# Four steps of the neighbourhood attention moved from the second branch's products to the third branch's gates

## The chip, the cores and the metric

The kernel runs on one core of one Trainium2 chip. The metric is the device time of one execution in microseconds. The kernel before takes 856.8 us (median of three runs, 856.2 to 856.81). One more execution was recorded by the hardware profiler; it took 857.18 us, and its span, from the first to the last instruction, is 855.4 us.

## What is computed

One layer of an encoder block on a sequence of 512 tokens with 1024 channels, all in float32. A projection of the normalised input feeds three token mixers. The second and third of the reference's mixers, and the merge, are what matters here:

```python
h = rms_norm(x, mix_norm_g)
proj = h @ w_in                      # mLSTM q,k,v,o,gates | NA q,k,v | memory q | merge gates
y_ml = mlstm_branch(...)
y_na = neighbourhood_attention(na_q, na_k, na_v, na_rpb)   # 8 heads of 64, 8 x 64 token grid
y_xa = memory_cross_attention(xa_q, mem_k, mem_v)
gates = sigmoid(merge_pre + b_merge_gate)
merged = g_ml * (y_ml @ w_br_ml) + g_na * (y_na @ w_br_na) + g_xa * (y_xa @ w_br_xa)
x = x + merged @ w_out
x = x + conv_glu_ffn(rms_norm(x))    # then a final norm
```

The neighbourhood attention lets a token look at all 8 rows and at 16 columns around it: scores with a learned bias, a softmax, and a weighted sum of values.

## The kernel before

**The products.** TensorE multiplies in float32 by three matmuls per product (`mm3`, L360 to L362): high part by high part, high by low, and low by high. The splits into high and low parts are made by ScalarE (ACT, L326: the rounded copy) and VectorE (DVE, L327: the rest). `proj` makes one 128 x 512 output tile from eight such triples, k = 0 to 7, so 24 matmuls, and may call a function after any k (its argument `at`). Weights come from HBM by SyncE's queue (`wr`, L239) three blocks ahead of their use, and are split one block ahead.

**The branches.** The merge runs in three rounds of a loop over `br`: br = 0 the mLSTM, br = 1 the memory attention, br = 2 the neighbourhood attention. Each round makes eight gates (`gate`, a `proj` and a tanh on ACT, L1264) and eight branch products of 12 matmuls each (four pairs), which DVE multiplies by the gate and adds to the merge (L1286, L1287). In rounds 0 and 1 two gates and a pair of products take turns. In round 2 all eight gates come first, then `drain` empties the attention's queue, then all products, which read the attention's result (`yh`, `yl`).

**The attention's steps.** While a round's matmuls run, a generator is advanced bit by bit (`step`; `half` is one step here, except for the mLSTM). `na_all` is advanced in rounds 1 and 2. It works on 16 tiles (a head and half of the columns each), called tile 0 to 15 here, in 39 steps. Two steps are one turn t. The first step of turn t does, in the order of the code: the scores of tile t on TensorE (four matmuls of 256 columns, L989 and L990) with their softmax (DVE maximum L994, ACT exponential L999, DVE reciprocal L1000, ACT scaling L1002); the values of tile t - 3 (four matmuls, L1023) and their sum (`store`: ACT L1039, DVE L1040 and L1041; for every fourth tile also the split into `yh` and `yl`, L1045 and L1046); the split of tile t - 2 (`parts`: two ACT copies L1011 and two DVE rests L1012); and the load of the transposed tile t - 1 (`turn_in`, one DMA `U<-td` of SyncE's queue, L179). The second step transposes tile t within blocks on DVE (L170) and stores it to HBM by four DMAs (`turn_out`, `td<-s`, L173). After every fourth tile `prep` splits the next pair of heads (L965 to L969), and `load_vwin` brings its values by 32 DMAs of GpSimd (POOL, L669). So a tile's values stand three turns behind its scores, and in between lie its softmax, a store to HBM, a load, and a split.

**The order.** The code's order is not the program's. A scheduling layer builds the five engines' instruction streams and places an instruction by when it expects it to be ready; the engines then run their streams in order, and wait at semaphores. The tiles named `U` and the split tiles (`w` of L1011) share a pool of six buffers (`EB`). The sums `mm` have four banks of PSUM, the attention's `at` four others.

Before the change a step is taken after k = 3 and after k = 7 of each gate, and after each branch product. Rounds 1 and 2 hold 16 + 8 and 16 of these places, so 40, all 12 large matmuls apart.

Of the kernel before, what the change touches and what calls it, by code (L numbers as in the profile page):

```python
# [20 lines left out]
KT = D // P  # L21
# [109 lines left out]
def hybrid_block(ctx, tc, xT, memT, wflat, vecs, gbias, nabias, out):  # L131
# [18 lines left out]
    def unit(dt=F32):  # L150
        return up.tile([P, UNIT], dt, tag="unit", name=nm("u"))

    def scr(n=512):
        return sp.tile([P, 512], F32, tag="scr", name=nm("s"))[:, :n]
# [4 lines left out]
    def mmps():  # L159
        return mmp.tile([P, 512], F32, tag="mm", name=nm("mm"))  # L160

    def atps():
        return atp.tile([P, 512], F32, tag="at", name=nm("at"))
# [168 lines left out]
    def weights(key):  # L332

        i, _, n = BINDEX[key]
        last = len(BLOCKS) - 1
        while st["raw"] <= min(i + RAW_AHEAD, DOWN0 + NSP - 1):
            emit_raw(st["raw"])
            st["raw"] += 1
        while st["late"] <= min(i + 9, last if i >= DOWN0 else DOWN0 + NSP + 3):
            emit_raw(st["late"])  # L340
            st["late"] += 1
        while st["sum"] <= min(i + 8, st["late"] - 1):
            emit_sum(st["sum"])
            st["sum"] += 1
        while st["diff"] <= min(i + 3, last):
            emit_diff(st["diff"])
            st["diff"] += 1
        while st["split"] <= min(i + (2 if st["split"] >= DOWN0 else SPLIT_AHEAD), last):
            emit_split(st["split"])
            st["split"] += 1  # L350
        while st["form"] <= min(i + 3, last):
            emit_form(st["form"])
            st["form"] += 1
        while st["diff"] <= min(i + 4, last):
            emit_diff(st["diff"])
            st["diff"] += 1
        return split.pop(i)

    def mm3(ps, lh, ll, rh, rl, start, stop):
        PE.matmul(ps, lh, rh, start=start, stop=False)  # L360
        PE.matmul(ps, lh, rl, start=False, stop=False)  # L361
        st["mm"] = PE.matmul(ps, ll, rh, start=False, stop=stop).ins  # L362
# [152 lines left out]
    def proj(key, XHs, XLs, n=S, bank=None, at={}):  # L515
        ws = weights(key)
        ps = (bank or mmps)()
        for k in range(KT):
            mm3(ps[:, :n], ws[k][0], ws[k][1], XHs[k], XLs[k], k == 0, k == KT - 1)
            if k in at:  # L520
                at[k]()
        return ps
# [53 lines left out]
    for f in range(4):  # L576
        ps = ps_k[f] if f < 2 else proj(("mlk", f), XH, XL)
# [44 lines left out]
    NH = [xn[k // 4][:, (k % 4) * S:(k % 4 + 1) * S] for k in range(KT)]  # L622
    NL = [xn[2 + k // 4][:, (k % 4) * S:(k % 4 + 1) * S] for k in range(KT)]
# [13 lines left out]
    for c, n in enumerate(TMW):  # L637
        pss = [(mmps if c % 2 else atps)() for _ in range(NT)]
        g = 2 if n == 512 else 4
# [10 lines left out]
        for t in range(NT):  # L650
            ps = pss[t]
# [10 lines left out]
    def load_vwin(hp):  # L662

        vw = unit(F32R)
        for b in range(4):
            for hf in range(2):
                i = 2 * b + hf
                for r in range(4):
                    G.dma_start(vw[r * 32:(r + 1) * 32, i * 256:(i + 1) * 256],  # L669
                                nav_v[hf, r, CW[b]:CW[b] + 32, hp * 256:(hp + 1) * 256])  # L670
        return vw
# [494 lines left out]
    def step(n=1):  # L1166
        quota[0] += n
        while quota[0] >= 1 and gens:
            try:
                next(gens[0])  # L1170
                quota[0] -= 1
            except StopIteration:
                gens.pop(0)
        if not gens:
            quota[0] = 0.0

    def half():

        step(0.5 if gens and gens[0].__name__ == "ml_all" else 1)

    def mid(at={}):

        return {**at, 2: lambda: step(RB / 2)}
# [6 lines left out]
    for f in range(4):  # L1190
        ps = proj(("xaq", f), NH, NL, at=mid())
# [3 lines left out]
    for f in range(4):  # L1195
# [6 lines left out]
        ps = proj(("o", f), NH, NL, at=mid())  # L1202
        if f == 0:
            so.append(unit())
        g = so[0][:, f * S:(f + 1) * S]
# [29 lines left out]
    for f in range(4):  # L1235
        ps = proj(("naq", f), NH, NL, at=mid())
        A.activation(nq[:, f * S:(f + 1) * S].rearrange("p (b r c) -> p b r c", r=ROWS, b=4), rv(ps), AF.Copy)
        step(RB / 2)
    for f in range(4):
        ps = proj(("nak", f), NH, NL, at=mid())  # L1240
# [8 lines left out]
    def drain(names):  # L1249
        while any(g.__name__ in names for g in gens):  # L1250
            step(1)

    for br in range(3):
        gi = (0, 2, 1)[br]
        if br == 0:
            ys[1] = [unit(F32R), unit(F32R)]
            gens.append(xa_all(xq, mk, mv, *ys[1]))
        if br == 1:
            vw0 = load_vwin(0)
            ys[2] = [unit(F32R), unit(F32R)]  # L1260
            gens.append(na_all(nq, nk, vw0, *ys[2]))
        def gate(f, t):
            ps = proj(("g", br, f), NH, NL, at={3: half, KT - 1: half})
            A.activation(t, ps, AF.Tanh, scale=0.5, bias=mgbh[:, gi * 8 + f:gi * 8 + f + 1])  # L1264
            return t

        if br == 2:
            tgu = [unit(), unit()]
            tgs = [gate(f, tgu[f // 4][:, f % 4 * S:(f % 4 + 1) * S]) for f in range(KT)]
        for fp in range(4):  # L1270
            tg = tgs[2 * fp:2 * fp + 2] if br == 2 else [gate(2 * fp + i, scr()) for i in range(2)]
            drain(tags[br])
            if br == 0 and not mg:
                mg.extend([unit(), unit()])
            yh, yl = ys[br]
            ws = weights(("br", br, fp))
            for i in range(2):
                f = 2 * fp + i
                ps = mmps()
                for k in range(4):  # L1280
                    ks, fs = slice(k * S, (k + 1) * S), slice(i * P, (i + 1) * P)
                    mm3(ps, ws[k][0][:, fs], ws[k][1][:, fs], yh[:, ks], yl[:, ks], k == 0, k == 3)
                if br == 0:
                    V.scalar_tensor_tensor(mgv(f), tg[i], 1.0, ps, op0=ALU.add, op1=ALU.mult)
                else:
                    V.scalar_tensor_tensor(tg[i], tg[i], 1.0, ps, op0=ALU.add, op1=ALU.mult)  # L1286
                    V.tensor_tensor(mgv(f), mgv(f), tg[i], op=ALU.add)  # L1287
                half()
    mhu = [unit(F32R) for _ in range(4)]
    GH = [mhu[k // 4][:, (k % 4) * S:(k % 4 + 1) * S] for k in range(KT)]  # L1290
    GL = [mhu[2 + k // 4][:, (k % 4) * S:(k % 4 + 1) * S] for k in range(KT)]
# [10 lines left out]
    for f in range(KT):  # L1302
        xr = scr()
        SY.dma_start(xr, xT[:, f, :])
        ps = proj(("out", f), GH, GL)
# [14 lines left out]
    for f in range(FT):  # L1320
# [38 lines left out]
        if 3 <= f < 11:  # L1359
            t, g = (f - 3) % NT, (f - 3) // NT  # L1360
            turns[t, g] = turn_out(x2v[g][:, :, t * P:(t + 1) * P])
        if 6 <= f < 14:
            t, g = (f - 6) % NT, (f - 6) // NT
# [99 lines left out]
    for n, key in enumerate(DOWN):  # L1463
        wh, wl = weights(key)
        work(2 if len(todo) > 2 else 1)
        if key[0] == "s":
            _, i, p = key
# [14 lines left out]
        _, g, j = key  # L1482
# [18 lines left out]
        for t in range(NT):  # L1501
            tsl = slice(t * P, (t + 1) * P)
            for c in ((slice(0, HC),) if t < last else (slice(0, M), slice(M, HC))):
                end = c.start > 0
                ps = px[t] if t < last else atps()[:, :M]
# [118 lines left out]
```

## Time and profile before

| | |
|---|---|
| median of 3 runs | 856.8 us |
| profiled execution | 857.18 us, span 855.4 us |
| TensorE busy | 847.4 us (99% of the span), 4010 matmuls |
| DVE, ACT, POOL busy | 603.4, 455.2 and 150.8 us |
| TensorE's granted clock | 0.998 |
| tile 0's scores, tile 15's values | at 312.5 us and 426.8 us |
| round 2, gates | from about 379 us to 430 us |
| HBM traffic | 155 GB/s over the span |

The page gives for each engine how long it was busy; a matmul's record lasts longer than its distance to the next one, because matmuls overlap, so TensorE's true pace is read from the starts in the timeline. A view of the waits lists who held up whom; the timeline gives every instruction with its start, its duration, and in brackets the idle time before it. Everything that the change moves lies between 312 and 455 us.

### The profile page before, as it was taken

What the parts mean: (1) busy time and instruction counts of PE and PEld (TensorE: products, weight loads), DVE (VectorE), ACT (ScalarE), POOL (GpSimd) and SP (SyncE); (2) the same over time, 40 slices, a digit from 0 to 9 for tenths busy, and PEclk for the clock granted to TensorE, in tenths of its full rate; (3) what the DMA queues carried; (4) which work ended last, traced back from release to release, by engine and by line L of the source; (5) the groups of instructions that cost most, each with busy time, mean ns of one, the idle gap of its engine ahead of it and who ended that gap; (6) DMA issues with size and microseconds to landing.
All of it is one profiled execution on the core that took longest, in us unless ns stands there. A gap on an engine that the chain in (4) does not pass through costs nothing.

```text
span 855.4 us, 12106 instructions
## 1 busy us (share of the span) xinstructions
PE 847.4 (99%) x4010; PEld 711.8 (83%) x4010; DVE 603.4 (71%) x1194; ACT 455.2 (53%) x956; POOL 150.8 (18%) x236
## 2 busy tenths in 40 slices
PE   9999999999999999999999999999999999999997
PEld 7898988888888888888888888888888888888886
DVE  7699677865458658998586547767766677766773
ACT  7465557775446648887644334434444444533442
POOL 2000100000102830554000211211111111210211
PEclk9999999999999999999999999999999999999999
DMA  8236736563335846788523442544422223845842
GB/s 273 87 113 212 235 113 201 179 208 105 120 122 170 225 142 203 227 228 236 177 96 110 148 160 88 163 156 148 147 99 99 95 93 113 236 119 148 247 107 98
DMA packets 78158, 133.63 MB, mean 156 GB/s; under 512 B 10888, under 2 KB 38024, under 8 KB 78096
## 3 DMA queue, kind: packets, MB, share of 16 engines
q1 hardware_dynamic: 68144, 122.22, 44.2%
q0 software_dynamic: 9664, 10.51, 6.2%
q8 instruction: 31, 0.51, 0.2%
q14 instruction: 31, 0.25, 0.1%
q10 hardware_dynamic: 288, 0.14, 0.1%
HBM read 117.21 MB, written 15.62 MB: 155 GB/s over the span
## 4 chain that ended last, share of the span: by engine, by line
PE 98%; DMA 1%; issue 0%; ACT 0%; SPq 0%; DVE 0%; POOLq 0%; POOL 0%; ACTq 0%
PE mm L361 28%; PE mm L360 28%; PE mm L362 28%; PE at L360 3%; PE at L361 3%; PE at L362 3%; PE at L1023 1%; PE at L856 1%; PE at L858 1%; PE at L840 1%; DMA wr<-wflat 1%; PE at L990 0%; PE at L989 0%; PE at L800 0%; PE mm L542 0%
## 5 line engine op out<-in xcount | busy, mean ns | idle before, releaser
L360 PE MATMUL mm<-u,w 128*128 128x512 f32 x859 | 336.3, 391 | 0.0
L362 PE MATMUL mm<-u,w 128*128 128x512 f32 x859 | 335.0, 390 | 0.0
L361 PE MATMUL mm<-u,w 128*128 128x512 f32 x859 | 334.9, 390 | 0.0
L326 ACT ACTIVATE w<-wr 128x512 fp32r<-128x512 f32 (+1 forms) x256 | 159.6, 627 | 134.7 <-PE mm L362 96.9
L327 DVE TENSOR_TENSOR w<-wr,w 128x512 fp32r<-128x512 f32 (+2 forms) x257 | 177.7, 695 | 69.3 <-ACT w L326 67.1
L362 PEld LDWEIGHTS mm<-u,w 128*128 128x128 f32 x859 | 161.3, 188 | 33.9 <-DVE w L327 0.3
L360 PEld LDWEIGHTS mm<-u,w 128*128 128x128 f32 x859 | 161.5, 188 | 32.5
L361 PEld LDWEIGHTS mm<-u,w 128*128 128x128 f32 x859 | 161.5, 188 | 32.1
L669 POOL DMA_DIRECT2D u<-nav_d x128 | 62.0, 497 | 102.6 <-PE at L1023 51.7
L1344 POOL TENSOR_TENSOR s<-s,rb 128x512 f32<-128x512 f32 x21 | 36.3, 1728 | 180.3 <-DVE s L1342 180.3
L360 PE MATMUL mm<-w,u 128*128 128x512 f32 x160 | 62.8, 393 | 0.0
L362 PE MATMUL mm<-w,u 128*128 128x512 f32 x160 | 62.4, 390 | 0.0
L361 PE MATMUL mm<-w,u 128*128 128x512 f32 x160 | 62.4, 390 | 0.0
L263 ACT ACTIVATE w<-u 128x512 fp32r<-128x512 f32 x48 | 30.1, 630 | 53.5 <-PE mm L362 39.3
L263 DVE TENSOR_TENSOR w<-u,w 128x512 fp32r<-128x512 f32 x48 | 33.1, 690 | 29.4 <-ACT w L263 29.0
L362 PEld LDWEIGHTS mm<-w,u 128*128 128x128 f32 x160 | 30.1, 188 | 6.3
L360 PEld LDWEIGHTS mm<-w,u 128*128 128x128 f32 x160 | 30.1, 188 | 6.0
L361 PEld LDWEIGHTS mm<-w,u 128*128 128x128 f32 x160 | 30.1, 188 | 6.0
L562 ACT ACTIVATE s<-pad,vec 128x512 f32<-128x512 f32 x30 | 24.4, 812 | 8.1 <-DVE pad L560 7.3
L366 ACT ACTIVATE u<-s 128x512 fp32r<-128x512 f32 x14 | 8.9, 632 | 36.1 <-DVE s L1352 36.1
L1313 POOL TENSOR_TENSOR acc<-acc,s 128x512 f32<-128x512 f32 x7 | 9.1, 1295 | 93.2 <-ACT s L1312 93.2
L563 DVE SCALAR_TENSOR_TENSOR s<-pad,vec,s 128x512 f32<-128x512 f32 x30 | 22.5, 749 | 3.7 <-ACT s L562 3.7
(308 smaller groups left out, 1176.7 us busy)
## 6 DMA issues: line engine op xcount, KB each, us to landing
wr<-wflat SPq DMA_DIRECT2D x124, 512.0 KB, 3.5
u<-wflat SPq DMA_DIRECT2D x48, 256.0 KB, 5.2
td<-s SPq DMA_DIRECT2D x172, 64.0 KB, 1.8
U<-td SPq DMA_DIRECT2D x41, 256.0 KB, 3.7
s<-xT SPq DMA_DIRECT2D x24, 256.0 KB, 4.1
nab<-nabias SPq DMA_DIRECT2D x16, 256.0 KB, 3.9
u<-nav_d POOLq DMA_DIRECT2D x128, 32.0 KB, 3.6
u<-wflat POOLq DMA_DIRECT2D x16, 256.0 KB, 7.4
```

Source lines behind the costliest of these rows:

```text
L263: chain[eng] = getattr({"V": V, "A": A, "G": G}[eng], what)(*a, **k).ins
L326: A.activation(h[:, u:v], src, AF.Copy)
L327: V.tensor_tensor(l[:, u:v], src, h[:, u:v].bitcast(F32), op=ALU.subtract)
L360: PE.matmul(ps, lh, rh, start=start, stop=False)
L361: PE.matmul(ps, lh, rl, start=False, stop=False)
L362: st["mm"] = PE.matmul(ps, ll, rh, start=False, stop=stop).ins
L366: A.activation(h, src, AF.Copy, scale=scale)
L562: A.activation(t1, pad[:, 0:512], AF.Identity, scale=vcol(w, i), bias=vcol(b, i))
L563: V.scalar_tensor_tensor(t1, pad[:, 1:513], vcol(w, n + i), t1, op0=ALU.mult, op1=ALU.add)
L669: G.dma_start(vw[r * 32:(r + 1) * 32, i * 256:(i + 1) * 256], nav_v[hf, r, CW[b]:CW[b] + 32, hp * 256:(hp + 1) * 256])
L1313: G.tensor_tensor(acc2, acc2, sq, op=ALU.add)
L1344: chain["G"] = G.tensor_tensor(c, c, rb2, op=ALU.mult).ins
```

## The change

Two places of the code. Round 2's gates take a step after k = 2, one after k = 5, and half a step after k = 7, so five steps per two gates instead of four. Round 1 takes a step only after the first product of each pair. Four steps leave round 1 (24 to 20) and four come into round 2 (16 to 20). Nothing is computed more or less, and nothing else is edited.

```diff
         def gate(f, t):
-            ps = proj(("g", br, f), NH, NL, at={3: half, KT - 1: half})
+            ps = proj(("g", br, f), NH, NL, at={3: half, KT - 1: half} if br < 2 else
+                      {2: half, 5: half, KT - 1: lambda: step(0.5)})
             A.activation(t, ps, AF.Tanh, scale=0.5, bias=mgbh[:, gi * 8 + f:gi * 8 + f + 1])
             return t
...
-                half()
+                if br != 1 or i == 0:
+                    half()
```

What the scheduling layer makes of it is shown at three places. A row gives a line, an operation, the tile written and the tiles read; the numbers in names count tiles as they are made, and `x2` is two equal rows.

The first place is TensorE's stream around the values of tile 11 (`at_4576` before, `at_4607` after). They follow the scores of tile 14 (L989, L990). Before:

```order
L989 MATMUL at_4560<-KS_4311,QS_4310 128x256
L990 MATMUL at_4560<-KS_4311,QZ_3318 128x256
L989 MATMUL at_4560<-KS_4311,QS_4310 128x256
L990 MATMUL at_4560<-KS_4311,QZ_3318 128x256
L1023 MATMUL at_4576<-w_4509,u_3957 128x256 x2
L1023 MATMUL at_4576<-w_4512,u_3957 128x256 x2
```

After, in the same place of the program:

```order
L989 MATMUL at_4591<-KS_4357,QS_4356 128x256
L990 MATMUL at_4591<-KS_4357,QZ_3318 128x256
L989 MATMUL at_4591<-KS_4357,QS_4356 128x256
L990 MATMUL at_4591<-KS_4357,QZ_3318 128x256
L360 MATMUL mm_4579<-u_626,w_4491 128x512
L361 MATMUL mm_4579<-u_628,w_4491 128x512
L362 MATMUL mm_4579<-u_626,w_4491 128x512
L360 MATMUL mm_4579<-u_627,w_4494 128x512
L1023 MATMUL at_4607<-w_4549,u_4006 128x256 x2
L361 MATMUL mm_4579<-u_629,w_4494 128x512
L1023 MATMUL at_4607<-w_4552,u_4006 128x256 x2
```

Both halves of the values moved behind four and five matmuls of the gate; the values of tiles 12 to 15 are moved back in the same manner, those of tiles 0 to 10 directly follow scores as before.

The second place is ACT's stream where tile 11 is split (the two L1011). Before:

```order
L1039 ACTIVATE acc_y_4355<-at_4501 64x256
L999 ACTIVATE s_4486,y_4495<-s_4486,y_4487 128x256 x2
L1011 ACTIVATE w_4509<-U_4440 128x2x128
L1002 ACTIVATE s_4486<-s_4486,y_4495 128x256 x2
L1011 ACTIVATE w_4512<-U_4440 128x2x128
L1264 ACTIVATE u_4262<-mm_4470,mgbh 128x512
L326 ACTIVATE w_4542<-wr_4387 128x512
```

After:

```order
L1039 ACTIVATE acc_y_4401<-at_4541 64x256
L999 ACTIVATE s_4526,y_4535<-s_4526,y_4527 128x256 x2
L1265 ACTIVATE u_4178<-mm_4497,mgbh 128x512
L1002 ACTIVATE s_4526<-s_4526,y_4535 128x256 x2
L1011 ACTIVATE w_4549<-U_4480 128x2x128
L1011 ACTIVATE w_4552<-U_4480 128x2x128
L326 ACTIVATE w_4576<-wr_4414 128x512
```

The split moved behind the tanh of a gate (L1265 is L1264 of before) and behind the softmax scaling of tile 13.

The third place is TensorE's stream at the last values, those of tile 15. Before they stand in the middle of the last gate (`mm_4794`), 12 matmuls ahead of its end:

```order
L361 MATMUL mm_4794<-u_628,w_4740 128x512
L362 MATMUL mm_4794<-u_626,w_4740 128x512
L1023 MATMUL at_4807<-w_4767,u_4317 128x256 x2
L1023 MATMUL at_4807<-w_4770,u_4317 128x256 x2
L360 MATMUL mm_4794<-u_627,w_4743 128x512
```

After, they stand in round 2's products (`mm_4838`, `mm_4853`, `mm_4876` are the first three):

```order
L361 MATMUL mm_4853<-u_3292,w_4788 128x512
L1023 MATMUL at_4813<-w_4773,u_4363 128x256 x2
L1023 MATMUL at_4813<-w_4776,u_4363 128x256 x2
L362 MATMUL mm_4853<-u_3291,w_4788 128x512
L360 MATMUL mm_4853<-u_3291,w_4788 128x512
```

and eight rows on, still in TensorE's stream of after:

```order
L361 MATMUL mm_4876<-u_3292,w_4832 128x512
L362 MATMUL mm_4876<-u_3291,w_4832 128x512
L360 MATMUL mm_4838<-u_3291,w_4791 128x512
L360 MATMUL mm_4853<-u_3291,w_4791 128x512
L360 MATMUL mm_4876<-u_3291,w_4832 128x512
L361 MATMUL mm_4838<-u_3292,w_4791 128x512
```

Ten large matmuls follow the values, and the next one, the L360 of `mm_4838`, is the first that reads what they end in, the last quarter of `yh` (`u_3291`); the L361 three places on reads that of `yl` (`u_3292`). Before, 12 matmuls of the gate and the nine that read the first three quarters lie between.

## The prediction

> **What bounds the kernel.** I read the page's first lines, then the waits of TensorE, then the timeline between the first scores (312 us) and round 2's products.
>
> ```profile
> span 855.4 us, 12106 instructions
> PE 847.4 (99%) x4010; PEld 711.8 (83%) x4010; DVE 603.4 (71%) x1194; ACT 455.2 (53%) x956; POOL 150.8 (18%) x236
> PE at L1023 <- PE at L990: 0.4, 1, 0.4
> ```
>
> TensorE is the bound: busy 99% of the span, and in all its waits one entry lies in the attention, 0.4 us ahead of the values (L1023). The change neither adds nor removes a matmul. So it can only take a wait out of TensorE's stream or put one in, and each lands on the span in full. First TensorE's pace, from starts:
>
> ```profile
> 330.31 0.28 PE L989 MATMUL at<-KS,QS 128*128 128x256 f32 x1
> ...
> 330.78 0.65 PE L1023 MATMUL at<-w,u 128*128 128x256 f32 x4
> 331.26 0.39 PE L360 MATMUL mm<-u,w 128*128 128x512 f32 x1
> ...
> 336.73 0.28 PE L989 MATMUL at<-KS,QS 128*128 128x256 f32 x1
> ```
>
> Four scores and four values take 331.26 - 330.31 = 0.95 us (0.119 each), and 24 large matmuls 336.73 - 331.26 = 5.47 us (0.228 each). Now the one wait:
>
> ```profile
> 374.59 0.33 SPq L179 DMA_DIRECT2D U<-td  x1
> ...
> 380.38 0.69 DVE L1286 SCALAR_TENSOR_TENSOR s<-s,mm 128x512 f32<-128x512 f32 x1
> 380.73 0.40 ACT L1011 ACTIVATE w<-U 128x256 fp32r<-128x256 f32 x1
> 381.10 0.69 DVE L1287 TENSOR_TENSOR u<-u,s 128x512 f32<-128x512 f32 x1
> 381.75 0.28 PE L989 MATMUL at<-KS,QS 128*128 128x256 f32 x1
> 381.99 0.40 ACT L1011 ACTIVATE w<-U 128x256 fp32r<-128x256 f32 x1
> 382.31 0.75 DVE L1012 TENSOR_TENSOR w<-U,w 128x256 fp32r<-128x256 f32 x2
> 382.83 1.08 PE L1023 MATMUL at<-w,u 128*128 128x256 f32 x4 [0.45 <-PE at L990]
> 383.75 0.40 PE L360 MATMUL mm<-u,w 128*128 128x512 f32 x1
> ```
>
> At turn 11 the values of tile 8 wait for their split (L1011, L1012). Its load (L179) was issued at 374.59 already; the split stood behind turn 10's softmax and round 1's products (L1286, L1287) in the streams of ACT and DVE. The eight small matmuls take 383.75 - 381.75 = 2.00 us instead of 0.95: this wait costs **1.05 us**. It is all that the change can win here.
>
> **The change, part by part.** *Removed: four steps from round 1.* A turn there is 24 large matmuls before; now it is 24 or 36. Turns with more room cannot wait more. Tile 8's scores now stand in round 1's last gate and its values in round 2's second, with a single step among the last products, so the DVE work of that place is spread. The order gives the tile 72 large matmuls (19.7 us) as before; tile 8's late split lay behind the products' DVE rows shown, so I take the 1.05 us as gone. Ends: 0 won to 1.05 won.
>
> *Added: four steps in round 2's gates, so turns there are shorter.* What a tile needs from its scores to its split, in an undisturbed place, tile 14:
>
> ```profile
> 402.06 0.28 PE L989 MATMUL at<-KS,QS 128*128 128x256 f32 x1
> 402.74 0.42 DVE L994 CUSTOM_DVE_ANT_0 s<-at,nab 128x256 f32<-128x256 f32 x1 [0.57 <-PE at L990]
> 404.71 0.50 ACT L999 ACTIVATE s<-s,y 128x256 f32<-128x256 f32 x1
> 406.22 0.89 ACT L1002 ACTIVATE s<-s,y 128x256 f32<-128x256 f32 x2
> 407.15 0.71 DVE L170 STREAM_TRANSPOSE s<-s 128x512 f32<-128x512 f32 x1
> 407.89 1.78 SPq L173 DMA_DIRECT2D td<-s  x4
> 411.16 0.33 SPq L179 DMA_DIRECT2D U<-td  x1
> ...
> 416.06 0.71 ACT L1011 ACTIVATE w<-U 128x256 fp32r<-128x256 f32 x2
> 417.17 0.74 DVE L1012 TENSOR_TENSOR w<-U,w 128x256 fp32r<-128x256 f32 x2
> ```
>
> That is 417.91 - 402.06 = 15.85 us, the lower bound of the need. The upper is a crowded place, tile 10:
>
> ```profile
> 375.31 0.28 PE L989 MATMUL at<-KS,QS 128*128 128x256 f32 x1
> 375.79 0.40 PE L1023 MATMUL at<-w,u 128*128 128x256 f32 x2
> ...
> 392.64 0.40 ACT L1011 ACTIVATE w<-U 128x256 fp32r<-128x256 f32 x1
> 394.54 0.38 DVE L1012 TENSOR_TENSOR w<-U,w 128x256 fp32r<-128x256 f32 x1
> ```
>
> 394.92 - 375.31 = 19.6 us. What the new order *gives*, counted in matmuls between scores and values (61 large and 28 small for tile 11: 13.9 + 3.3 = 17.2 us): tiles 9 and 10 16.3 us, tile 11 17.2, tile 12 17.7, tile 13 16.3 (its second half 17.7), tile 14 17.4, tile 15 18.7. Before it was 19.7 for all of 3 to 12. So room falls by up to 3.4 us, to within 0.5 us of the lower bound.
>
> Which need applies? The engines' load says nearer to the upper:
>
> ```profile
> 336.00:354.60 18.60, 18.60 (x94) 15.80 (x94) 16.87 (x46) 15.46 (x39) 3.60 (x8) 1.00 0.67 204
> 397.00:408.50 11.50, 11.50 (x56) 9.60 (x56) 8.81 (x25) 8.93 (x24) 0.85 (x3) 1.00 0.88 259
> ```
>
> (columns: stretch, length, busy PE, PEld, DVE, ACT, POOL, clock, DMA share, GB/s). In round 2 DVE is busy 8.81 of 11.50 us, ACT 8.93, both some 77%. A turn there is now 19.7 large matmuls on the mean (59 triples over nine turns), 5.4 us instead of 6.4; the attention's work per us grows by a sixth, the weights' and gates' does not, so I estimate 85 to 90% for both, about what DVE has in round 1 (16.87 of 18.60). So I follow tile 11 through the streams, from its scores at 0; tile 12's scores stand at 5.05, tile 13's at 11.45.
>
> ```profile
> L965 ACT ACTIVATE QS<-u x8: 616/628/633, 282.8 to 383.5; 64x512 fp32r<-64x512 f32 x8
> L1264 ACT ACTIVATE u<-mm,mgbh x8: 667/690/691, 387.4 to 430.2; 128x512 f32<-128x512 f32 x8
> ```
>
> ACT first does three copies for the next heads (L965 and its like, 0.63 each), the attention's sum (0.4), two exponentials (0.50 each, 1.1 with their reads), tile 9's split (0.7) and the scaling (0.9): done at 5.5, transposed (0.71) at 6.2. SyncE's stream has tile 11's load behind the first store of tile 12, whose transposition, by the same addition, is done at 11.55; so the load is issued at 12.0 and lands in 3.8:
>
> ```profile
> U<-td SPq DMA_DIRECT2D x4, 256.0 KB, 3.8
> td<-s SPq DMA_DIRECT2D x16, 64.0 KB, 2.5
> ```
>
> That is 15.8. But the split now stands on ACT behind tile 13's exponentials, a gate's tanh and the scaling. Tile 13's scores end at 11.95; DVE gets to its maxima behind tile 10's split and a weight's rest at 13.0; exponentials end at 15.45, the tanh (0.69) at 16.1, the scaling at 17.0. The first half of the split is ready at 17.0 + 0.4 + 0.4 = 17.8 to 17.95, and with tile 10's wait before it due at 17.4. Tile 11 waits about 0.6 to 0.75 us. The same walk gives 0.2 us for tile 10, 0.55 for tile 12's second half, 0.25 for tile 13, nothing for 9, 14 and 15: **1.75 us**. Ends: 0 (need 15.85 everywhere) to 6.1 (tiles 9, 12 and 15, each of whose scores stand just ahead of the values of the one before, have 16.3 + 17.7 + 18.7 = 52.7 us, against three times 19.6). The row nearest in place is tile 10's, the row nearest in work, without products, tile 14's; the walk lies between them, at a need of 16.5 to 18.2.
>
> [...]
>
> *The weights' split (L326, L327) and the weight loads* lie in the same streams a gate ahead of their use (5.47 us); the walk has them ready over 2 us early: nothing, unless tiles wait longer than that.
>
> *GpSimd's loads of the values of the last heads.*
>
> ```profile
> 392.86 4.86 POOL L669 DMA_DIRECT2D u<-nav_d  x10 [3.33 <-issue]
> u<-nav_d POOLq DMA_DIRECT2D x31, 32.0 KB, 3.7
> ```
>
> Released by tile 7's values (375.79 above), the last lands at 397.7 + 3.7 = 401.4, some 25 us later. The half that tile 12 needs comes first; the rest is needed by tile 13, 31 us after tile 7's values in the new order. Nothing; 2 us if it took a third longer.
>
> *The end.* Before, the chain behind the last values had 21 matmuls of cover; now ten.
>
> ```profile
> 426.80 0.64 PE L1023 MATMUL at<-w,u 128*128 128x256 f32 x4
> 429.30 0.64 ACT L1045 ACTIVATE u<-acc_y 128x512 fp32r<-128x512 f32 x1 [1.27 <-DVE acc_y L1041]
> 429.97 0.69 DVE L1046 TENSOR_TENSOR u<-acc_y,u 128x512 fp32r<-128x512 f32 x1 [0.70 <-ACT u L1045]
> ```
>
> From the first values to `yh` it is 3.14 us, to `yl` 3.86. Covered are 0.48 + 10 x 0.228 = 2.75 and 3.4: **0.4 us** of wait. Ends: 0 to 1.0, the latter if a weight's copy on ACT (0.63 like L965), which now stands ahead of `yh`, is in its way.
>
> **The sum.** 857.18 - 1.05 + 1.75 + 0.4 = 858.3 us for the profiled execution, which lies 0.4 us above the median of the runs; so **857.9 us** against 856.8.
>
> **Rivals.**
> *A: the tiles need no more than tile 14 needed, 15.85 us.* For it: without round 1's products DVE has no L1286 and L1287 in the way. Against it: the load of 85 to 90%, and splits that now stand behind a later tile's softmax. Time: 856.8 - 1.05, and up to 0.4 for the end, so 855.8 to 856.2.
> *B, slower: the chain from scores to split becomes the pace.* Its place is turns 12 to 18, its price up to the 6.1 us above, so up to 856.8 - 1.05 + 6.1 + 0.4 = 862.3, the middle 860.5. It decides from a need of 17.5 us on, where two waits of 1.2 us each (tiles 10 and 13, or 9 and 12) outweigh the win by the 1.7 us that can be measured. For it: tile 10's 19.6, and a DMA share of 0.88 already. Against it: each wait gives the next tile more room.
> *C: the wait of 1.05 us stays*, because tile 8 is late for its load and not for the products; then 858.9. Against it: the load's row, 374.59 + 3.8 = 378.4, lies 2 us ahead of the copy.
>
> **How the numbers follow.** Times within 0.2% (1.7 us) cannot be told from no change here. My case (new waits of 1 to 3.5 us, 856.7 to 859.3) has 0.50, of which 0.16 lies above 858.5; A 0.25, of which 0.04 is for a gain that I cannot see in this trace; B 0.20; C 0.05, 0.02 of it slower. Faster 0.04; the same 0.34 + 0.21 + 0.03 = 0.58; slower 0.16 + 0.20 + 0.02 = 0.38. The range goes from 0.4 us under A's lower end to above B's middle: 855.4 to 861.2.
>
> **What would show it.** After: no idle time ahead of L1023 at turn 11; short idle entries, each under 1 us, ahead of the values of tiles 10 to 13 (turns 13 to 16), released by DVE's L1012; one of about 0.4 us ahead of the first product's last quarter, released by L1045. I am wrong if these sum to under 0.5 us, or to over 4, or if a weight's L327 releases TensorE.

## The result, and the profile after

The changed kernel takes 859.79 us (median of six runs, 859.42 to 860.53), the kernel before 856.8 beside it: a ratio of 1.0037, 95% interval 1.0026 to 1.0048, so 2.2 to 4.1 us slower. In a second set of runs the ratio was 1.0038 (1.0026 to 1.0051). The time lies 1.9 us above the 857.9 us that were forecast. The range held it, but the likeliest case's own range, which ended at 859.3, did not.

The page's first lines and two entries of its waits (engine and line, what it waited for: us in all, times, longest). The profiled execution took 860.53 us, the longest of the six:

```profile
span 858.8 us, 12107 instructions
PE 848.8 (99%) x4010; PEld 710.6 (83%) x4010; DVE 603.3 (70%) x1194; ACT 455.5 (53%) x956; POOL 150.8 (18%) x236
PE at L1023 <- issue: 2.0, 1, 2.0
PE at L1023 <- DVE w L1012: 0.4, 1, 0.4
```

No engine has more instructions; one entry of 2.0 us ahead of values is new, and one of 0.4 us has another releaser. The timeline of TensorE at turn 11, at the values of tile 9 (turn 12), and at those of tile 11:

```profile
390.31 0.28 PE L990 MATMUL at<-KS,QZ 128*128 128x256 f32 x1
390.43 0.64 PE L1023 MATMUL at<-w,u 128*128 128x256 f32 x4
390.91 0.39 PE L360 MATMUL mm<-u,w 128*128 128x512 f32 x1
...
395.38 0.28 PE L990 MATMUL at<-KS,QZ 128*128 128x256 f32 x1
397.64 1.05 PE L1023 MATMUL at<-w,u 128*128 128x256 f32 x4 [1.98 <-issue]
398.53 0.40 PE L360 MATMUL mm<-u,w 128*128 128x512 f32 x1
...
410.55 0.47 PE L1023 MATMUL at<-w,u 128*128 128x256 f32 x2 [0.43 <-DVE w L1012]
```

Tile 8's values follow its turn's scores at once: the wait of before is gone. At tile 9 the five matmuls from 395.38 take 398.53 - 395.38 = 3.15 us instead of 0.58, so 2.57 are lost. "issue" there is TensorE's wait for the split, as ACT's and DVE's rows show:

```profile
382.76 0.33 SPq L179 DMA_DIRECT2D U<-td  x1
387.73 0.73 ACT L1011 ACTIVATE w<-U 128x256 fp32r<-128x256 f32 x2 [1.00 <-DMA U<-td]
388.18 0.76 DVE L1012 TENSOR_TENSOR w<-U,w 128x256 fp32r<-128x256 f32 x2 [0.73 <-ACT w L1011]
388.97 0.42 DVE L994 CUSTOM_DVE_ANT_0 s<-at,nab 128x256 f32<-128x256 f32 x1
390.44 0.51 ACT L999 ACTIVATE s<-s,y 128x256 f32<-128x256 f32 x1 [0.92 <-DVE y L996]
390.82 0.33 SPq L179 DMA_DIRECT2D U<-td  x1
...
396.19 0.49 ACT L999 ACTIVATE s<-s,y 128x256 f32<-128x256 f32 x1
396.69 0.70 ACT L1011 ACTIVATE w<-U 128x256 fp32r<-128x256 f32 x2
397.12 0.76 DVE L1012 TENSOR_TENSOR w<-U,w 128x256 fp32r<-128x256 f32 x2
```

Read from below: tile 9's copies (396.69) have no idle time ahead; they stood behind tile 11's exponentials (396.19) at the end of a row of ACT work without a gap from 390.44 on. That row began late, with tile 10's exponentials; these waited for its maxima (388.97), which stood behind tile 8's split (388.18), whose load (382.76) landed 5.0 us after its issue.

How far behind the attention is, the distance from a tile's first score on TensorE to its first maximum on DVE tells best. Tiles 9, 12 and 13:

```profile
379.14 0.28 PE L989 MATMUL at<-KS,QS 128*128 128x256 f32 x1
381.38 0.42 DVE L994 CUSTOM_DVE_ANT_0 s<-at,nab 128x256 f32<-128x256 f32 x1
...
395.02 0.28 PE L989 MATMUL at<-KS,QS 128*128 128x256 f32 x1
399.43 0.41 DVE L994 CUSTOM_DVE_ANT_0 s<-at,nab 128x256 f32<-128x256 f32 x1
404.02 0.28 PE L989 MATMUL at<-KS,QS 128*128 128x256 f32 x1
405.43 0.42 DVE L994 CUSTOM_DVE_ANT_0 s<-at,nab 128x256 f32<-128x256 f32 x1
```

The lag grows from 0.68 (tile 8) to 2.24, 3.41, 3.67 and 4.41 us at tile 12; TensorE's waits then give it time, and at tile 13 it is 1.41. Before, it was at most 2.44 in the same stretch and fell back to 0.67.

At the end, the first product waits for `yh` (0.28) and `yl` (0.27); in starts each costs 0.1 us:

```profile
437.89 0.53 PEld L360 LDWEIGHTS mm<-u,w 128*128 128x128 f32 x3 [0.28 <-ACT u L1045]
438.70 0.19 PEld L361 LDWEIGHTS mm<-u,w 128*128 128x128 f32 x1 [0.27 <-DVE u L1046]
```

### The profile page after: what moved, and what is told of

It is laid out like the page before. It is cut to its first block, busy times and chain, and to the rows that moved or that the text cites. A ratio compares the mean times of both kernels' runs of the same rounds, so it can differ in the third digit from the quotient of the medians.

```text
span 858.8 us, 12107 instructions
## 1 busy us (share of the span) xinstructions
PE 848.8 (99%) x4010; PEld 710.6 (83%) x4010; DVE 603.3 (70%) x1194; ACT 455.5 (53%) x956; POOL 150.8 (18%) x236
## 4 chain that ended last, share of the span: by engine, by line
PE 93%; DMA 3%; DVE 2%; issue 1%; ACT 1%; SPq 0%; POOLq 0%; POOL 0%; DVEq 0%; ACTq 0%
PE mm L362 26%; PE mm L361 26%; PE mm L360 26%; PE at L360 3%; PE at L361 3%; PE at L362 3%; DMA U<-td 1%; PE at L1023 1%; PE at L856 1%; DMA td<-s 1%; PE at L858 1%; PE at L840 1%; DMA wr<-wflat 0%; PE at L800 0%; PE at L989 0%
## 5 line engine op out<-in xcount | busy, mean ns | idle before, releaser
L360 PE MATMUL mm<-u,w 128*128 128x512 f32 x859 | 335.7, 391 | 0.0
L361 PE MATMUL mm<-u,w 128*128 128x512 f32 x859 | 334.6, 390 | 0.0
L327 DVE TENSOR_TENSOR w<-wr,w 128x512 fp32r<-128x512 f32 (+2 forms) x257 | 177.8, 696 | 60.7 <-ACT w L326 58.5
L360 PEld LDWEIGHTS mm<-u,w 128*128 128x128 f32 x859 | 161.2, 188 | 32.7 <-ACT u L1045 0.3
L361 PEld LDWEIGHTS mm<-u,w 128*128 128x128 f32 x859 | 161.3, 188 | 32.6 <-DVE u L1046 0.3
L360 PE MATMUL mm<-w,u 128*128 128x512 f32 x160 | 62.7, 392 | 0.0
L361 PE MATMUL mm<-w,u 128*128 128x512 f32 x160 | 62.3, 389 | 0.0
L360 PEld LDWEIGHTS mm<-w,u 128*128 128x128 f32 x160 | 30.1, 188 | 6.1
L361 PEld LDWEIGHTS mm<-w,u 128*128 128x128 f32 x160 | 30.1, 188 | 6.0
```

The costliest lines, as they stand in the source:

```text
L327: V.tensor_tensor(l[:, u:v], src, h[:, u:v].bitcast(F32), op=ALU.subtract)
```

## The experiments

The loss at a tile is what its four values and the matmul ahead of each group take from start to start, beyond 0.227 us for a large and 0.117 for a small one, in each kernel's one profiled execution. "Half clock" is what TensorE lost to a lower clock behind a wait, in us, and is explained under the hardware below.

| kernel | time to that of before (95%) | tile 8 | tile 9 | tile 10 | tiles 11 to 15 | half clock |
|---|---|---|---|---|---|---|
| before | 1 | 1.06 | 0 | 0 | 0 | |
| changed | 1.0037 (1.0026 to 1.0048) | 0 | 2.57 | 0.19 | 1.33 | |
| changed, second profile | 1.0038 (1.0026 to 1.0051) | 0 | 2.36 | 0 | 0.85 | 1.4 |
| round 1 thinned only | 1.0013 (1.0004 to 1.0022) | 0 | 0 | 0 | 0.27 | |
| round 2 dense only | 1.0020 (1.0011 to 1.0030) | 0.73 | 0 | 0.06 | 1.01 | |
| no loads of the last values | 1.0061 (1.0048 to 1.0075) | 0 | 1.67 | 0 | 0.87 | |
| heads' copies on GpSimd | 1.0061 (1.0048 to 1.0074) | 0 | 2.94 | 0 | 0.96 | 1.0 |
| tile 9's split first | 1.0060 (1.0047 to 1.0074) | 0 | 0.34 | 2.32 | 0.75 | 1.6 |
| dense from the third gate on | 1.0033 (1.0021 to 1.0046) | 0 | 0 | 1.75 | 1.33 | |
| tile 10's maxima first | 1.0033 (1.0021 to 1.0045) | 0 | 1.72 | 0 | 0.98 | |
| two additions left out | 1.0040 (1.0028 to 1.0053) | 0 | 1.50 | 0 | 1.00 | |
| values one place later | 1.0037 (1.0023 to 1.0051) | 0 | 0 | 0.94 | 2.96 | |
| last step left out | 0.9994 (0.9985 to 1.0003) | 0 | 0 | 0 | 0 | |
| one step moved to the front | 0.9996 (0.9987 to 1.0004) | 0 | 0 | 0 | 0 | |

**The two halves.** Against the changed kernel: round 2's gates as before,

```diff
-            ps = proj(("g", br, f), NH, NL, at={3: half, KT - 1: half} if br < 2 else
-                      {2: half, 5: half, KT - 1: lambda: step(0.5)})
+            ps = proj(("g", br, f), NH, NL, at={3: half, KT - 1: half})
```

> Half of the change: round 1 with 20 places, round 2's gates as before (two per gate); the three steps left over are taken by drain after the last gate. Tile 9 has room for 19.7 us instead of 16.3. Theory S: no wait at tile 9, and none at turn 11 (the 1.05 us of before stays gone); at the end tile 15 has room for 15.3 us only, so a wait of 0.5 to 1.5 us ahead of its values, and 0.4 to 1 us for yh; time 856.5 to 858.3. Theory R (it is round 1's thinning, which puts tiles 8 and 9 where the products end): tile 9 or its neighbours wait 1 us or more in this kernel too; time 858 to 860.

and round 1 as before:

```diff
-                if br != 1 or i == 0:
+                if True:
```

> The other half: round 1 as before (24 places), round 2's gates with five steps per two gates, so the attention ends four places earlier. Tile 9 has room for 19.0 us, tiles 10 to 13 for 17.0, 17.2, 16.3 and 17.0. Theory S: the wait of 1.05 us at turn 11 (tile 8) is there as before; tile 9 waits under 0.3; tiles 10 and 12 wait 0.3 to 1.0 each; nothing at the end; time 857.2 to 858.8. Theory R: the density of round 2 costs nothing by itself: no wait over 0.3 us behind turn 11; time 856.6 to 857.0.

Theory S holds in both traces in the main, with smaller losses than it expected: neither half has the one at tile 9; density costs about 1.1 us at tiles 10 to 13, the most at tile 11 (0.54), which theory S had not named; thinning alone costs the attention 0.27 at tile 15 and nothing at `yh`, where 0.4 to 1 was expected. Only together do they put tile 9's scores right behind the last products *and* its values into short turns. The times say it less sharply: +1.1 us for thinning alone, which I see only in part (in its profile the wait for the first loads of the kernel is 0.6 us longer, and the stretch behind the last matmul 0.3; and in each of its eleven executions some 2.1 us of the time lie outside the span, against 1.8 in nearly all of the kernel before). By the ratios the halves, 0.13 and 0.20%, nearly add up to the whole, 0.37%, so that both are needed together is shown for tile 9's loss in the traces, not for the time.

**Is it the transfers?** Without GpSimd's loads for tiles 12 to 15:

```diff
-                vws[i // 4 + 1] = load_vwin(i // 4 + 1)
+                vws[i // 4 + 1] = load_vwin(i // 4 + 1) if i < 8 else vws[i // 4]
```

> The changed kernel without GpSimd's 32 loads of the last two heads' values: tiles 12 to 15 multiply with the values of the heads before (left out: these loads, so the last quarter of the attention is not the reference's). TensorE's and ACT's streams keep their order. In the changed kernel these loads ran from 377.55 to 397.1 us, and the load of tile 8 (U<-td, issued at 382.76) landed only when ACT's copy could start at 387.73, 5.0 us later, against a median of 3.7. Theory D (transfers): this late load starts the delay of tile 9; without the loads tile 8's load takes 3.7 us or less, and the wait of 2.0 us ahead of tile 9's values falls under 0.5; time 857.0 to 857.9. Theory S (streams): tile 9 is late because ACT works without a gap for 6.25 us (390.44 to 396.69) ahead of its split, with room for 16.3 us only; the wait falls by at most the 1.0 us of the late load and stays 1.0 to 2.0; time 858.3 to 859.8.

```profile
386.81 0.71 ACT L1011 ACTIVATE w<-U 128x256 fp32r<-128x256 f32 x2
397.01 1.05 PE L1023 MATMUL at<-w,u 128*128 128x256 f32 x4 [1.08 <-issue]
```

Tile 8's copies start 0.9 us earlier (386.81 for 387.73), and tile 9 loses 0.9 us less, but still 1.67: theory S, as far as the trace goes. The time, 861.56 us, missed both theories, since the kernel's end became 2 us longer (under the hardware below).

**Is it ACT's work?** The copies for the next heads on GpSimd:

```diff
-                A.activation(q2[own], qn[own], AF.Copy)
-                A.activation(k2[own], kn[own], AF.Copy)
-                A.activation(q2[oth], qn[own], AF.Copy)
+                G.tensor_copy(q2[own], qn[own])
+                G.tensor_copy(k2[own], kn[own])
+                G.tensor_copy(q2[oth], qn[own])
```

> The changed kernel with the three copies of the next heads (L965 to L967) made by GpSimd instead of ACT, for all heads. Two sets of them stand in ACT's streams near tile 9, the second from 393.45 to 395.26 us, 1.9 us just ahead of its split. Theory S (streams): tile 9's split starts up to 1.9 us earlier, and its wait of 2.0 us falls to 0 to 0.7; time 857.0 to 858.5, unless GpSimd's copies delay the scores of tile 12 (a wait ahead of L989). Theory D (transfers): the load of tile 8 stays late at 387.7 us, and the wait stays over 1.5 us; time 859 to 860.

```profile
394.62 0.51 ACT L999 ACTIVATE s<-s,y 128x256 f32<-128x256 f32 x1 [1.01 <-DVE y L996]
395.62 0.71 ACT L1011 ACTIVATE w<-U 128x256 fp32r<-128x256 f32 x2
```

Theory S in this form falls, and theory D's sign (a load until 387.7) did not come either: its copies of tile 8 started at 386.7. Up to tile 9 ACT had 1.9 us less to do and stood idle for 1.0 us instead, since tile 11's exponentials still waited for its maxima on DVE. Tile 9's copies came 0.4 us earlier behind its scores (17.2 for 17.5), but its rests on DVE started 1.05 us behind them instead of 0.43, and the loss rose to 2.94. Taking work off one engine did not help here, where two hand each other the work. The time, 861.41 us, missed both theories too: the half clock stands in this kernel's profile, and its five executions have granted clocks of 0.995 to 0.997, where the six of the changed kernel's first set have 0.998 or 0.999.

**Is it one order?** Tile 9's copies ahead of all of turn 11 on ACT (`st["cp"]` is the last of them, and `issue_after` orders ACT's instructions; the next heads' second set of copies is wrapped alike). The scheduling layer built the other streams anew, but TensorE's order is the changed kernel's up to tile 11's values:

```diff
+                if t == 11:
+                    pts[9] = parts(us.pop(9))
+                with tc.issue_after(st["cp"]) if t == 11 else ExitStack():
                     sm = scores(t, ops, bt)
...
+                with tc.issue_after(st["cp"]) if t == 11 else ExitStack():
                     out(t - 3)
```

> The changed kernel with one order forced: in turn 11 ACT issues tile 9's two split copies ahead of tile 11's exponentials, of the second set of copies for the next heads, and of tile 8's sum, which all stood ahead of them. Nothing else is edited. Theory O (order: the split's load had landed, and the copies stood behind later work in ACT's stream): the copies start at about 394.6 us (load issued at 390.8, landing in 3.7) instead of 396.7, and TensorE's loss at tile 9's values, 2.6 us, falls to 0.3 to 1.0; time 857.8 to 859.0, or 0.5 us more if tile 11's softmax, now behind, makes tile 11 later. Theory L (late load: tile 9's own load lands only when the copies started): the copies wait for the load, and the loss stays over 2 us; time 859.3 to 860.3.

In this kernel's lines, L1012 and L1013 are the split, L1024 the values:

```profile
394.64 0.73 ACT L1012 ACTIVATE w<-U 128x256 fp32r<-128x256 f32 x2 [0.72 <-DMA U<-td]
395.86 0.97 PE L1024 MATMUL at<-w,u 128*128 128x256 f32 x4
403.98 0.50 PE L1024 MATMUL at<-w,u 128*128 128x256 f32 x2 [1.21 <-DVE w L1013]
405.05 0.51 PE L1024 MATMUL at<-w,u 128*128 128x256 f32 x2 [0.57 <-DVE w L1013]
```

The load landed at 394.6, as theory O said, and tile 9's loss fell to 0.34. But tile 10 now loses 2.32 instead of 0.19. The lateness was passed on, and the time, 862.32 us, missed both theories: it rose, by the half clock (1.6 us) and by a wait of some 0.7 us at 538 us, far behind the attention, among others.

**Is it the place?** Round 2's first two gates as before:

```diff
-at={3: half, KT - 1: half} if br < 2 else
+at={3: half, KT - 1: half} if br < 2 or f < 2 else
```

> The changed kernel with round 2's first two gates as before (steps after k = 3 and 7), and five steps per two gates from the third on: 20 + 19 places. Tile 9 has room for 19.0 us instead of 16.3, tiles 10 to 15 for 17.0, 17.2, 16.3, 17.4, 17.2 and 16.7. Theory P (place: 16.3 us are too little only right behind round 1's products, where DVE and ACT carry their work along): nothing is lost at tile 9; tiles 10 to 15 lose 0.1 to 0.7 each, 1.0 to 1.8 in sum; time 857 to 858.5. Theory N (need: a tile with room for 16.3 us loses 2 us or more wherever it stands): the loss moves to tile 12; time 859 to 860.5.

```profile
404.05 0.48 PE L1023 MATMUL at<-w,u 128*128 128x256 f32 x2 [0.83 <-DVE w L1012]
405.39 0.51 PE L1023 MATMUL at<-w,u 128*128 128x256 f32 x2 [0.40 <-DVE w L1012]
```

Both theories miss: tile 9, with 19.0 us, loses nothing, but tile 10, with 17.0, loses 1.75, and tile 12, with the least room, 0.19. In the half that is dense only, tile 10 had 17.0 as well and lost 0.06; there tile 8's wait (0.73) fell between its scores and its values and gave it time. With room, wait and loss, tile 10 took 17.0 + 1.75 = 18.75 us here and 17.0 + 0.73 + 0.06 = 17.8 there. So neither one place nor the room alone sets the loss; what a tile takes goes with the lag that it arrives with: tile 10's maxima came 2.2 us behind its scores here, 1.1 there. In the same way tile 10's wait gave tile 12 time here.

**Two links of the chain.** Tile 10's maxima ahead of tile 8's rests on DVE:

```diff
-                V.tensor_tensor_reduce(smv[:, j, :], ps[:, js], bt[:, js], 1.0, 2.0 * NEG, ALU.add, ALU.max,
-                                       accum_out=mx[:, j:j + 1])
+                st["mx"] = V.tensor_tensor_reduce(smv[:, j, :], ps[:, js], bt[:, js], 1.0, 2.0 * NEG, ALU.add, ALU.max,
+                                       accum_out=mx[:, j:j + 1]).ins
...
-                pts[t - 2] = parts(us.pop(t - 2))
+                with tc.issue_after(st["mx"]) if t == 10 else ExitStack():
+                    pts[t - 2] = parts(us.pop(t - 2))
```

> The changed kernel with one order forced on DVE: tile 8's split rests (L1012) are issued behind tile 10's maxima (L994) instead of ahead of them; TensorE's and ACT's streams keep their order. In the changed kernel DVE stood idle for 0.73 us ahead of these rests, because tile 8's load landed at 387.7 us, and tile 10's maxima, whose scores had been there since 386.1, started at 388.97. Theory C (chain: this wait passes from tile 10's maxima to its exponentials, through ACT's unbroken row of work to tile 11's exponentials and to tile 9's split): the maxima start 1.5 us earlier, and TensorE's loss at tile 9's values falls from 2.6 to 0.9 to 1.6 us, the losses of tiles 9 to 15 together from 4.1 to 2.0 to 3.0; time 858.0 to 859.0. Theory B (pace: the attention's work through ACT and DVE cannot keep up with these turns, and a wait taken from one tile comes back at the next): tile 9 loses less, tiles 10 and 11 more, the sum stays 3.5 to 4.5; time 859.3 to 860.5.

and round 1's last two additions left out:

```diff
-                    V.tensor_tensor(mgv(f), mgv(f), tg[i], op=ALU.add)
+                    if (br, fp) != (1, 3):
+                        V.tensor_tensor(mgv(f), mgv(f), tg[i], op=ALU.add)
```

> The changed kernel without the two last additions of round 1's products to the merge (L1288, 0.69 us each, left out: the memory branch's share in two of eight blocks). All other instructions keep their order. In the changed kernel one of them stood ahead of tile 9's maxima, which came 2.24 us behind its scores. Theory D2 (DVE's leftovers of the products make tile 9 late): the maxima come 0.7 to 1.4 us earlier, the loss of 2.6 us at tile 9's values falls under 1.9 us; time 858.5 to 859.3. Theory C (the loss comes through tile 8's split and the softmax of tiles 10 and 11, and tile 9's own load has landed 2 us before its copies): the loss stays 2.2 to 2.8 us; time 859.3 to 860.2.

The traces lean to theory C in the first (tile 9 loses 1.72, a little over its range; tiles 9 to 15 together 2.71) and to theory D2 in the second (1.50). But in the second, tile 8's copies, which waited for their load, also came 1.1 us earlier behind its scores than in the changed kernel, so the fall is not the additions' alone; and neither median (859.45 and 859.47) differs from the changed kernel's by what can be told. The second profile of the unedited kernel, below, has a sum of 3.2 where the first had 4.1. Inconclusive, apart from this: no single wait was worth the loss.

**Is it the pace?** The values of tiles 9 to 13 one step later:

```diff
-            if t - 3 in pts:
+            if t - 3 in pts and not 12 <= t <= 16:
                 out(t - 3)
...
                 ds[t] = turn_out(by4(sm))
+            if 12 <= t <= 16:
+                out(t - 3)
```

> The changed kernel with the values of tiles 9 to 13 taken in the second step of their turn instead of the first, one place later; all steps stand where they did. Room between scores and values: tiles 9 to 14 have 19.7, 17.7, 18.3, 19.7, 17.2 and 18.3 us, against 16.3, 16.3, 17.2, 17.7, 16.3 and 17.4 in the changed kernel, where what they took (room and loss) was 18.9, 16.5, 17.9, 17.9, 16.4 and 17.4. Theory R (room against need: each tile behind round 1's products needs 16.5 to 19 us, whatever stands where, and loses what its room lacks): nothing is lost at tile 9, 0 to 1.2 us at tile 10, under 0.3 us at each other tile, the sum of tiles 9 to 15 falls from 4.1 to 0.3 to 1.5; time 856.0 to 857.6. Theory B (pace: the work of a turn on ACT and DVE takes longer than these turns, so lateness only grows and the later place is used up): losses of 1 us or more at tiles 10 to 13, a sum of 2.5 or more; time 858.5 to 860.

First and last scores and maxima of tiles 10 to 15, the waits ahead of values, and the engines in that stretch (columns as in the prediction):

```profile
385.12 0.28 PE L989 MATMUL at<-KS,QS 128*128 128x256 f32 x1
413.16 0.28 PE L989 MATMUL at<-KS,QS 128*128 128x256 f32 x1
388.20 0.43 DVE L994 CUSTOM_DVE_ANT_0 s<-at,nab 128x256 f32<-128x256 f32 x1
417.38 0.42 DVE L994 CUSTOM_DVE_ANT_0 s<-at,nab 128x256 f32<-128x256 f32 x1
...
403.93 0.51 PE L1023 MATMUL at<-w,u 128*128 128x256 f32 x2 [0.66 <-DVE w L1012]
420.79 0.56 PE L1023 MATMUL at<-w,u 128*128 128x256 f32 x2 [0.99 <-DVE w L1012]
385.10:413.20 28.10, 27.30 (x138) 22.94 (x137) 22.41 (x63) 22.08 (x56) 8.50 (x19) 1.00 0.77 209
```

Theory B by the sum, though only one tile lost over 1 us, and the time, 860.39 us, lies 0.4 above its range. Nothing is lost at tile 9, but the lag, with no wait there to shorten it, goes on to 4.66 us at tile 14; tile 10 loses 0.94 and tile 13 1.98: the losses of tiles 9 to 15 are 3.9 in all, as in the changed kernel (4.1 and 3.2 in its two profiles), and the time is the same. The attention's maxima come every (417.38 - 388.20) / 5 = 5.84 us, TensorE's turns, without the 1.35 us lost between, every (28.04 - 1.35) / 5 = 5.34. DVE and ACT are busy only 80 and 79% of that stretch. The rest is mostly one waiting for the other: in the waits of that stretch ACT stands 4.5 us for maxima of DVE and 1.2 for tile loads, DVE 5.1 us for ACT.

**The changed kernel once more**

> The changed kernel once more, unedited, beside the same runs of the kernel before: a second profile of it, to tell what a single profile shows from what stays. Theory F (fixed: the order of the streams sets the loss): 2.4 to 2.7 us at tile 9, 0.6 to 0.7 at tile 11, as in the first profile, whose execution was the longest of six. Theory V (varying: the loss at tile 9 follows when tile 8's load lands, which the other transfers shift by up to 1.4 us): 1.4 to 2.4 us at tile 9, with tile 8's copies earlier than 17.1 us behind its scores by about as much. Time 859.4 to 860.2 in either.

```profile
397.48 1.25 PE L1023 MATMUL at<-w,u 128*128 128x256 f32 x4 [1.62 <-issue]
```

Theory V, by a little: tile 9 loses 2.36, just inside its range, with tile 8's copies 0.4 us earlier, and tile 11 loses 0.29, under theory F's 0.6. So a loss at one tile in one profile is good to some 0.4 us only, and the sum of tiles 9 to 15 (4.1 and 3.2) to 0.9, while tile 9's stays the largest.

**Two versions that take the one wait of before away**, both against the kernel before:

```diff
-                half()
+                if not (br == 1 and fp == 3 and i == 1):
+                    half()
```

> The kernel before with one place less: no step after the very last product of round 1, so all later steps come one place later (39 places for 39 steps), with round 2's gates as before. Tiles 8, 9 and 10 have room for 22.4 us, all others what they had. If the 1.05 us at turn 11 come from the crowd of round 1's last products, as the prediction held: no wait at tile 8, none elsewhere, the end as before; time 855.4 to 856.2. If they come from tile 8's late load or from density alone: a wait of 0.5 us or more stays at tile 8; time 856.3 to 857.

and, with this edit too,

```diff
-at={3: half, KT - 1: half})
+at={3: half, KT - 1: half} if (br, f) != (1, 0) else {1: half, 3: half, KT - 1: half})
```

> The kernel before with one step moved: none after the last product of round 1, one more in round 1's first gate (after k = 1), so that all tiles up to tile 8 come one place earlier and the rest stays. Tiles 8, 9 and 10 have room for 22.4 us, as in the kernel with one place less, but the attention ends where it did before, so the end is not lost (there 0.3 us at yh and yl). If the gain at turn 11 and the loss at the end are all that counts: no wait at tile 8, nothing lost at the end, time 855.4 to 856.0. If the earlier places of tiles 3 to 7 bring new waits, or the gain is taken back elsewhere: 856.2 to 857.2.

In both, no tile waits, as expected; the second loses nothing at the end either, the first 0.3 us. Yet the times, 856.41 and 856.36 us, are only 0.5 and 0.3 us lower, with intervals that include no change, and both lie above the range that went with no wait. Either beats the changed kernel; whether one beats the kernel before is open.

## Why the prediction was right or wrong

The range held the time by its width, not by the walk: the walk's sum missed by 1.9 us, and the time lies where rival B had its share. By the sign that it gave for being wrong (waits of over 4 us in sum) the forecast fails in the first profile, with 4.1 + 0.2, and not in the second, with 3.2 + 0.2; the sign of waits under 1 us each fails in both, at tile 9.

- *The removed wait, -1.05*: gone, as said. Its size is that of one execution, 0.4 us above the median. The two versions bound what it is worth on the median: 0.5 us (-0.3 to 1.3) and 0.3 (-0.3 to 1.1).
- *The new waits, +1.75*: the step that failed. Tiles 10 to 13 were to lose 0.2, 0.6 to 0.75, 0.55 and 0.25 and lost 0.19, 0.67, 0.23 and 0.14 (second profile: 0.01, 0.29, 0.11, 0.20). Tile 9, put at nothing, lost 2.57 and 2.36: its need was not 16.3 us or less but 397.64 - 379.14 = 18.5. Tile 15, put at nothing too, lost 0.25 and 0.24. In all it was 4.1 and 3.2 for 1.75. The walk began at tile 11, so it took tile 9 over in an undisturbed state. Before's trace had the row, a few us from those that I quoted:

```profile
368.89 0.28 PE L989 MATMUL at<-KS,QS 128*128 128x256 f32 x1
385.69 0.42 ACT L1011 ACTIVATE w<-U 128x256 fp32r<-128x256 f32 x1
387.00 0.40 ACT L1011 ACTIVATE w<-U 128x256 fp32r<-128x256 f32 x1
```

  The first of tile 9's copies came 16.8 us behind its scores, the second 18.1; with the 0.95 us from copies to values that the changed kernel shows, the first alone makes 17.75, against room for 16.3. (Its room was 19.7 then, so the rows say what tile 9 took, not the least that it needs.)
- *85 to 90% busy*: it was 86% for DVE in the changed kernel from 379.1 to 395 us (13.69 of 15.90) and 80% for ACT (12.76). What was read from it, a need nearer to the upper end of 19.6, was right for tile 9; the walk that followed did not use it there. In the kernel with the values one place later, at 80%, the two engines already fell behind by half a microsecond a tile.
- *Rival B* is nearest to what happened, by its own sign (need 18.5, over 17.5) and by its place, at 4.1 and 3.2 of its 6.1 us, though tile 9 alone bore most of it, and not tiles 9, 12 and 15 alike. What I held against it, that each wait gives the next tile room, is true (the lag of 4.41 fell to 1.41), and a likely reason why it stopped there. It had deserved more than 0.20. A and C did not come.
- *The end, +0.4*: 0.2, by the two waits named.
- *The weights' splits*: L327 never released TensorE in the changed kernel's waits of this stretch, as said.
- *GpSimd's loads*: none of their readers waited, but they may not be free: from issue to copies tile 8's load took 387.73 - 382.76 = 4.97 us with them, at most 3.9 in the one profile without. Since it varied by 1.1 us between kernels that have them, this is not shown.
- *The tile loads, put at 3.8 us in the walk*: the ten of the changed kernel between 366 and 432 us, from issue to landing, have a median of 3.7 us:

```profile
DMA to landing us min/median/max: 2.7/3.7/5.4
```

## What to carry to other kernels

Ask of a pipelined side job not only whether its engines have idle time, but how far the first step behind TensorE lags from tile to tile: here a lag that grew meant that the job's pace had become the bound, and a wait that was taken from one tile came back at a later one (2.32 us at tile 10, 1.98 at tile 13). Read the need of each moved tile at its own place in the old trace, and compare it with the new room, before costing any as undisturbed. Do not thin one stretch and crowd the next at the place where the first one's leftovers are worked off.

## What the runs showed of the hardware

**Half clock behind waits of about 2 us.** In three of the profiled executions TensorE ran on at half its clock behind a wait. Second profile of the changed kernel, TensorE's timeline and the granted clock by stretch; the kernel with the heads' copies on GpSimd; and the one with tile 9's split first:

```profile
398.53 0.63 PE L360 MATMUL mm<-u,w 128*128 128x512 f32 x1
...
401.50 0.39 PE L361 MATMUL mm<-u,w 128*128 128x512 f32 x1
395.50:398.50 3.00, 1.38 (x8) 1.06 (x7) 2.48 (x7) 2.98 (x10) 1.19 (x4) 0.93 0.82 190
398.50:401.50 3.00, 3.00 (x8) 2.34 (x8) 2.87 (x10) 1.01 (x4) 0.00 (x0) 0.51 0.42 111
401.50:405.00 3.50, 3.50 (x17) 2.90 (x16) 1.51 (x4) 3.50 (x11) 0.00 (x0) 1.00 0.73 200
```

```profile
397.18 1.24 PE L1023 MATMUL at<-w,u 128*128 128x256 f32 x4 [2.20 <-issue]
394.60:397.10 2.50, 0.38 (x4) 0.16 (x2) 2.45 (x7) 2.48 (x8) 1.81 (x4) 0.98 0.85 166
397.10:400.10 3.00, 2.92 (x9) 2.56 (x10) 2.99 (x10) 0.92 (x3) 1.26 (x3) 0.50 0.83 204
400.10:405.00 4.90, 4.90 (x24) 4.05 (x23) 2.01 (x5) 4.12 (x11) 3.71 (x9) 0.97 0.91 266
```

```profile
404.00:408.00 4.00, 3.43 (x12) 2.68 (x13) 3.38 (x11) 2.44 (x8) 0.00 (x0) 0.73 0.78 258
408.00:412.00 4.00, 4.00 (x19) 3.32 (x18) 2.67 (x8) 2.61 (x7) 0.00 (x0) 0.84 0.16 45
412.00:420.00 8.00, 8.00 (x40) 6.57 (x40) 5.29 (x17) 6.06 (x15) 0.00 (x0) 1.00 0.71 209
```

In the first of the three, seven large matmuls took 401.50 - 398.53 = 2.97 us instead of 1.59: behind 1.62 us of idling another 1.4 were lost. If the clock was 0.5 while it was low, the rows make that 3.4 us in each of the three (2 x (0.07 x 3.00 + 0.49 x 3.00) in the first). The length of the wait alone does not tell whether the clock falls: it did behind 1.62 and 2.20 us of idling, and behind 1.21 and 0.57 us at the two halves of one tile's values, but in the first profile of the changed kernel, behind 1.98 us, it stayed at 1.00. One execution of the same kernel has the half clock and another has not; what decides it, the runs do not show.

**A longer end.** Without GpSimd's 32 loads, the last stores were issued 1.25 us earlier than in the changed kernel (855.25), and the span still ended 0.7 us later (row: the last two stores, the first of them issued at 854.00):

```profile
854.00 0.93 SPq L1452 DMA_DIRECT2D out<-s  x2
span 859.5 us, 12049 instructions
```

From there to the span's end it took 5.5 us, against 858.8 - 855.25 = 3.6. Counted from the very last issue it is 5.0 us here and 3.0 in the kernel before, in the changed kernel, and with the heads' copies on GpSimd; nothing in the trace tells why.
